# Pairs of 256-column products become single 512-column products

## The chip, the cores and the metric

The kernel runs on one core of a Trainium2 chip. Its time is what the device takes for one launch, in microseconds. Three runs of the kernel before took 2214.0, 2215.96 and 2220.0 us (median 2215.96). One more execution was profiled; all rows below come from it.

## The reference

Two small transformers run one after the other on 256 tokens of width 1024, all in fp32. The first has two layers; each is a gated feed-forward block, a token mixing block and a second feed-forward block:

```
h = h + 0.5*g1*swiglu(modulate(rms_norm(h)), wg, wu, wd)        # d_ff 2816
h = h + g2*token_mixing(modulate(rms_norm(h)), w_in, ...)       # two attentions, a gate, w_o
h = h + 0.5*g3*swiglu(modulate(rms_norm(h)), wg', wu', wd')
```

The second takes this result and a second stream of 256 context tokens. Its layer 0 runs retention and a gated scan on both streams, an output product, and an MLP of width 4096 with squared ReLU, again on both. Its layer 1 is a windowed attention and such an MLP on the first stream alone. The shifts, scales and gates (18 vectors of the first, 16 of the second part) are products of three conditioning vectors with weights of their own.

## The kernel before

**Tiling.** Activations are kept transposed: a list of four tiles, each with two blocks of 128 features (k) by 256 tokens. Every fp32 operand is split into two rounded halves, `h` and `l`, and each product is three products (`mm3`, line 849): hh, hl, lh. A weight tile of 512 KB is loaded into an `f4` slot by SP's queue, rounded by ScalarE (`CAST r<-f`) and subtracted by VectorE (`TENSOR_TENSOR r<-f,r`), so that it occupies two `r4` slots (`wload`, line 825). `wcols` (line 835) loads 256 columns of a weight as two tiles of four k.

**Two kinds of product.** `tr_product` (line 854) holds 128 weight columns still and lets 256 tokens pass: its result is transposed, one 128x512 PSUM bank for 256 weight columns. `nat_product` (line 864) holds 128 tokens still and lets 256 weight columns pass; t numbers the two blocks of 128 tokens. Both have 24 products of 256 columns for one half of a bank (8 k times 3). The down products (`down`, `half`) already pass 512 columns. PSUM has four banks `gu` and four `acc`.

**Stages.** The labels are 0ffn1, 0mix, 0ffn2, 1ffn1, 1mix, 1ffn2 (first part, `feed` and `mixing`), ret (`retention_gla`), out (`half`), jmlp (`joint_mlp`), win (`window`), mlp (`feed`). A stage ends in a tail: for each t the residual, the norm and four transposes, mostly on VectorE. The next stage starts with products by token block, which need only t = 0 while the tail of t = 1 runs: `by_tile` in the feed-forwards (two slices p of 256 columns) and the queries in mixing and win. In ret and jmlp the streams are `"c"` (context) and `"x"`; each passes through every weight tile in its own products.

**Order.** The engines' orders are not the code's. Each call is recorded as an operation with a cost; products into one bank join up to 1400 ns. A planner (`Plan.schedule`, line 255) then lays the operations out over PE, ACT, DVE, POOL and SP with modelled times, takes the earliest-recorded ready one first, and gives each tile one of the slots in `SLOTS`. What is printed by `order` is that fixed sequence. On the chip an engine never leaves its sequence. Background units (`bg`: `ma<-mw`, one 512 KB tile for the conditioning vectors) are spread over the stages.

Because every call goes through line 506, all instructions have that line, and the rows are told apart by tile names: `r` split halves, `f` raw weights, `b` half-width work tiles, `ma`/`mw` conditioning, `resx` the residual.

Of the kernel before, what the change touches and what calls it, by code (L numbers as in the profile page):

```python
# [15 lines left out]
ALU = mybir.AluOpType  # L16
# [13 lines left out]
SLOTS = {"r4": 26, "f4": 7, "mw": 2, "ma": 3, "b2": 17, "p256": 4, "p128": 5, "p16": 12, "pb": 2}  # L30
# [9 lines left out]
VERBOSE = False  # L40

# [394 lines left out]
class _Engine:  # L436
# [3 lines left out]
    def __getattr__(self, what):  # L440
# [3 lines left out]
        def call(*args, **kw):  # L444
# [62 lines left out]

            plan.record(eng, issue, outs, ins, dur, nbytes, table, share)
# [67 lines left out]
def two_blocks_kernel(ctx: ExitStack, tc: tile.TileContext, A: dict, out: bass.AP, dumps=None):  # L576
# [248 lines left out]
    def wload(ap, a, b):  # L825
        l = r4()[:, : a * b].rearrange("p (a b) -> p a b", a=a)
        r = f4()[:, : a * b].rearrange("p (a b) -> p a b", a=a)
        load(r, ap)
# [13 lines left out]

    def ahead(*which):

        for W, c0 in which:
            ws = wcols(W, c0)
            stash[W.tensor.name, W.offset, c0] = ws
# [6 lines left out]
    def tr_product(ps, nT, ws, nk=KT):  # L854

        for b in range(2):
            o = ps[:, b * T : b * T + T]
            c = slice(b * P, b * P + P)
            for k in range(nk):
                wh, wl = ws[k // 4]  # L860
                nh, nl = nT(k)
                mm3(o, wh[:, k % 4, c], wl[:, k % 4, c], nh, nl, k == 0, k == nk - 1)

    def nat_product(o, nT, ws, t):

        tt = slice(t * P, t * P + P)
        for k in range(KT):
            wh, wl = ws[k // 4]
            nh, nl = nT(k)
            mm3(o, nh[:, tt], nl[:, tt], wh[:, k % 4, :], wl[:, k % 4, :], k == 0, k == KT - 1)  # L870
# [12 lines left out]
    def kpairs(tiles):  # L883


        def f(k):
            c = slice((k % 2) * T, (k % 2) * T + T)
            return tiles[k // 2][0][:, c], tiles[k // 2][1][:, c]

        return f  # L890
# [118 lines left out]
    def gated(nT, wg, wu):  # L1009


        def whole(p):
            pg, pu = gu(), gu()
            tr_product(pg, nT, wcols(wg, p * 256))
            tr_product(pu, nT, wcols(wu, p * 256))
            sg, hd = b2(), b2()
            nc.scalar.activation(sg, pg, AF.Silu)
            nc.vector.tensor_mul(hd, sg, pu)
            return kpairs([split(hd, 0.5)])

# [12 lines left out]

        return lambda p: by_tile(p) if p < NAT else whole(p)

    def squared(nT, w1):
        def whole(p):
            ps = gu()
            tr_product(ps, nT, wcols(w1, p * 256))
            hd = b2()  # L1040
            nc.scalar.activation(hd, ps, AF.Relu)
            nc.scalar.activation(hd, hd, AF.Square)
            return kpairs([split(hd)])

        def by_tile(p):
            ws = wcols(w1, p * 256)
            h = pair()
            for t in range(2):
                ps = gu()
                nat_product(ps[:, 0:T], nT, ws, t)  # L1050
                hd = pl([P, T])
                nc.scalar.activation(hd, ps[:, 0:T], AF.Relu)
                nc.scalar.activation(hd, hd, AF.Square)
                put([h], 0, t, transposed(gu(), hd))
            return kpairs([h])

        return lambda p: by_tile(p) if p < 2 else whole(p)
# [144 lines left out]
    def mixing(l, nT, m, rate, before, tail, after=()):  # L1202
# [21 lines left out]
        def dv(c):  # L1224
            ps = gu()
            ws = wcols(W, 1792 + c * 256)
            for t in range(2):
                nat_product(ps[:, t * T : t * T + T], nT, ws, t)
            nc.scalar.copy(vd[:, :, c * 256 : c * 256 + 256], ps.rearrange("p (t c) -> p t c", t=2))
# [222 lines left out]
    def retention_gla(nT, lgam, between):  # L1452
# [6 lines left out]
        def pr_T(c0):  # L1459
            ws = wcols(W, c0)  # L1460
            ps = {}
            for n in both:
                ps[n] = gu()
                tr_product(ps[n], nT[n], ws)
            return ps

        def pr_N(c0):

            v = {n: [b2(), b2()] for n in both}
            for c in range(2):  # L1470
                ws = wcols(W, c0 + c * 256)
                for n in both:
                    ps = gu()
                    for t in range(2):
                        nat_product(ps[:, t * T : t * T + T], nT[n], ws, t)
                    for t in range(2):
                        copy = nc.scalar.copy if t == 0 else nc.vector.tensor_copy
                        copy(v[n][t][:, c * 256 : c * 256 + 256], ps[:, t * T : t * T + T])
            return v

        def silu(c0):

            g = {}
            for b in range(2):
                ps = pr_T(c0 + b * 256)
                for n in both:
                    g[n, b] = b2()
                    nc.scalar.activation(g[n, b], ps[n], AF.Tanh, scale=0.5)
                    nc.vector.scalar_tensor_tensor(g[n, b], g[n, b], 1.0, ps[n], ALU.add, ALU.mult)
# [173 lines left out]
        pq = pr_T(1536)  # L1663
        qb, kb = {}, {}
        for n in both:
            qb[n] = b2()
            nc.scalar.mul(qb[n], pq[n], 0.125)
        pk = pr_T(1792)
        for n in both:
            kb[n] = b2()  # L1670
            nc.scalar.copy(kb[n], pk[n])
# [138 lines left out]
    def joint_mlp(nT, w1, w2, x, gates, before, tail, after, stats):  # L1810

        hid = {}

        def hidden(*ps):
            ws = {p: wcols(w1, p * 256) for p in ps}
            for n in ("c", "x"):
                for p in ps:
                    o = gu()
                    tr_product(o, nT[n], ws[p])
                    hd = b2()  # L1820
                    nc.scalar.activation(hd, o, AF.Relu)
                    nc.scalar.activation(hd, hd, AF.Square)
                    hid[n, p] = split(hd)
# [5 lines left out]
        for r in range(4):  # L1829
            mine = {n: kpairs([hid[n, 4 * r + i] for i in range(4)]) for n in ("c", "x")}  # L1830
# [10 lines left out]
    def window(nT, ctx, consts, before, tail, after):  # L1841
# [9 lines left out]
        def queries(half, t, ws):  # L1851
            pq[half, t] = acc()
            for c in range(2):
                nat_product(pq[half, t][:, c * 256 : c * 256 + 256], nT, ws[c], t)
# [26 lines left out]
        ws = [wcols(W, c * 256) for c in range(2)]  # L1881
# [14 lines left out]
        def more_queries():  # L1896
            ws = [wcols(W, 512 + c * 256) for c in range(2)]
            for t in range(2):
                pq[1, t] = gu()
                for c in range(2):  # L1900
                    nat_product(pq[1, t][:, c * 256 : c * 256 + 256], nT, ws[c], t)
# [122 lines left out]
    for l in range(2):  # L2024
# [9 lines left out]
        feed(gated(kpairs(nT), A["ffn_wg"][l, 0], A["ffn_wu"][l, 0]), A["ffn_wd"][l, 0], 11, RATE if l else FIRST, before, closing(*keys, n2), [(A["w_in"][l], 0), (A["w_in"][l], 256)], lead=0 if l else LEAD)  # L2034
# [4 lines left out]
        mixing(l, kpairs(n2), hold["m"], RATE / 3, lambda: get(*keys), closing(*keys, n3), [(A["ffn_wg"][l, 1], 0), (A["ffn_wu"][l, 1], 0)])  # L2039
# [6 lines left out]
        else:  # L2046
            cT, xT = new_T(), new_T()

            def before():
# [6 lines left out]
                for t in range(2):  # L2056
                    normed(cT, t, xc[t], None, V["Csc1_0"], V["Csh1_0"])
# [8 lines left out]
            def tail(t, accs):  # L2066
# [3 lines left out]
                normed(xT, t, xs[t], r, V["Xsc1_0"], V["Xsh1_0"])  # L2070
# [4 lines left out]
        feed(gated(kpairs(n3), A["ffn_wg"][l, 1], A["ffn_wu"][l, 1]), A["ffn_wd"][l, 1], 11, RATE, before, tail, [(A["ffn_wg"][1, 0], 0), (A["ffn_wu"][1, 0], 0)] if l == 0 else [(A["ev_w_in_2"][0], 0), (A["ev_w_in_2"][0], 256)])  # L2075
# [6 lines left out]
    y = retention_gla({"c": kpairs(cT), "x": kpairs(xT)}, hold["lgam"], lambda: bg(1))  # L2082

    def ln_tail(n, t, st, nxt, G, SH, g, b):
        mean, r = moments(st)
        normed(nxt, t, x[n][t], r, G, SH, mean=mean)
        affine(x[n][t], mean, r, g, b)
# [7 lines left out]
    nxt, maps = {}, {}  # L2095
    for n in both:
# [3 lines left out]
        nxt[n] = new_T()  # L2100
    half(y, A["ev_w_out_2"][0], 0, 1, ALPHA, x, gates, lambda n, t: ln_tail(n, t, stats[n, t], nxt[n], *maps[n], g, b), [(A["mlp_w1_2"][0], 0)], stats)
# [5 lines left out]
    nT = {n: kpairs(nxt[n]) for n in both}  # L2107
# [53 lines left out]
    def tail(t, accs):  # L2161
        st = new_stats()
        residual(xs[t], accs, V["Xg1_1"], t, ALPHA, stats=st)
        ln_tail("x", t, st, last, *lastmap["m"], *lastmap["l"])

    window(kpairs(nx2["x"]), ctx_keys, consts, before, tail, [(A["mlp_w1_2"][1], 0), (A["mlp_w1_2"][1], 256)])
# [59 lines left out]
```

## Time and profile before

| | |
|---|---|
| median of three runs | 2215.96 us (2214.0 to 2220.0) |
| profiled execution | 2215.32 us, span 2213.5 us |
| mean granted TensorE clock | 0.984 |
| TensorE busy | 2109.6 us (95%) |
| VectorE, ScalarE busy | 1594.7 us (72%), 999.8 us (45%) |
| read from HBM | 447.11 MB, 203 GB/s over the span |

Read it from the engine that is nearly always busy: its busy share by stage, then what one of its instructions costs where it never waits (start of one row to the start of the next), then the places where it does wait and for whom.

### The profile page before, as it was taken

Reading aid. Unit: us, or ns where it says so; the run is one execution under the profiler, and the core shown is the slowest. Engines: PE = TensorE matmul, PEld = TensorE weight load, DVE = VectorE, ACT = ScalarE, POOL = GpSimd, SP = SyncE. Lnnn points to the kernel's source line nnn. Section 1 sums busy time; section 2 is a strip of 40 time slices with the busy share of each in tenths; the row PEclk is TensorE's granted clock in tenths of the full one; section 3 lists DMA queues with packets and bytes.
Section 4 is the critical chain, followed back from the end, with each engine's and each line's share of the span. In section 5 each row is a group of like instructions: output and inputs, shape, how many; then the busy total and the mean of one; then the engine's idle time right before and its main releaser. Section 6 shows DMA issues by size and latency. Waiting matters only on the chain. (4 is left out here: it accounts for less than half of the span.)

```text
span 2213.5 us, 37030 instructions
## 1 busy us (share of the span) xinstructions
PE 2109.6 (95%) x14996; PEld 1911.0 (86%) x14996; DVE 1594.7 (72%) x2111; ACT 999.8 (45%) x1525; POOL 53.7 (2%) x51
## 2 busy tenths in 40 slices
PE   7999799999999999999999899979999999989998
PEld 4999798899989998988998798868998898978997
DVE  6777887886687669899789965559653536878545
ACT  3544355454444445565445326423333332365552
POOL 0000100000000000000000010000000000000000
PEclk8999999999999999999999999989999999999999
DMA  9988867698868874776797543244642423244661
GB/s 347 353 265 319 267 203 238 216 303 272 271 224 295 273 240 143 230 246 224 252 315 239 165 144 99 100 137 133 205 150 86 162 86 126 73 139 130 205 215 55
DMA packets 282084, 450.73 MB, mean 204 GB/s; under 512 B 17164, under 2 KB 203692, under 8 KB 281912
## 3 DMA queue, kind: packets, MB, share of 16 engines
q1 hardware_dynamic: 281912, 448.37, 61.4%
q8 instruction: 117, 1.92, 0.4%
q14 instruction: 55, 0.45, 0.1%
HBM read 447.11 MB, written 1.20 MB: 203 GB/s over the span
## 5 line engine op out<-in xcount | busy, mean ns | idle before, releaser
L506 PE MATMUL gu<-r,r 128*128 128x256 f32 (+1 forms) x9776 | 1224.0, 286 | 8.7 <-DVE r L506 5.3
L506 PEld LDWEIGHTS gu<-r,r 128*128 128x128 f32 (+1 forms) x9776 | 1196.6, 193 | 30.9 <-issue 12.0
L506 ACT CAST r<-f 128x1024 fp32r<-128x1024 f32 x545 | 566.5, 1051 | 651.7 <-PE acc L506 133.8
L506 DVE TENSOR_TENSOR r<-f,r 128x1024 fp32r<-128x1024 f32 x545 | 652.4, 1221 | 207.4 <-PE gu L506 80.6
L506 PE MATMUL acc<-r,r 128*128 128x512 f32 (+3 forms) x3408 | 721.8, 375 | 21.7 <-ACT b L506 12.8
L506 PEld LDWEIGHTS acc<-r,r 128*128 128x128 f32 (+1 forms) x3408 | 574.7, 189 | 138.3 <-ACT b L506 14.3
L506 DVE SCALAR_TENSOR_TENSOR ma<-mw,sc_all,ma 128x1024 f32<-128x1024 f32 x252 | 320.3, 1281 | 106.6 <-DMA mw<-in_ada_w 60.7
L506 ACT CAST r<-gu 128x256 fp32r<-128x256 f32 (+2 forms) x130 | 42.9, 387 | 150.7 <-PE gu L506 150.7
L506 DVE TENSOR_TENSOR r<-b,r 128x512 fp32r<-128x512 f32 (+1 forms) x74 | 46.1, 632 | 82.4 <-ACT r L506 82.1
L506 POOL TENSOR_TENSOR p<-p,mhalf 128x1 f32<-128x1 f32 (+2 forms) x42 | 51.0, 1217 | 2154.9 <-DVE p L506 2154.9
L506 ACT ACTIVATE b<-gu 128x512 f32<-128x512 f32 x92 | 54.9, 596 | 103.1 <-PE gu L506 102.9
L506 PE MATMUL gu<-ident,b 128*128 128x128 f32 (+1 forms) x448 | 64.6, 287 | 38.0 <-DVE b L506 35.3
L506 PEld LDWEIGHTS gu<-ident,b 128*128 128x128 f32 (+1 forms) x448 | 46.6, 143 | 53.5 <-DVE b L506 46.9
L506 DVE TENSOR_TENSOR b<-acc,b 128x512 f32<-128x512 f32 (+1 forms) x82 | 54.9, 673 | 22.1 <-PE acc L506 21.0
L506 DVE TENSOR_TENSOR b<-b,b 128x512 f32<-128x512 f32 (+2 forms) x97 | 63.1, 668 | 7.4 <-DMA b<-mod_Csc 2.2
L506 ACT ACTIVATE b<-acc,p 128x256 f32<-128x256 f32 (+1 forms) x96 | 51.6, 548 | 23.0 <-DVE p L506 18.2
L506 ACT ACTIVATE ma<-mw,sc_all 128x1024 f32<-128x1024 f32 x36 | 41.5, 1152 | 40.2 <-DMA mw<-in_ada_w 21.5
L506 DVE SCALAR_TENSOR_TENSOR r<-b,r 128x512 fp32r<-128x512 f32 x44 | 30.3, 689 | 38.0 <-ACT r L506 38.0
L506 DVE TENSOR_TENSOR r<-gu,r 128x256 fp32r<-128x256 f32 (+2 forms) x130 | 49.6, 430 | 5.5 <-ACT r L506 5.2
L506 ACT CAST r<-b 128x512 fp32r<-128x512 f32 (+1 forms) x74 | 41.6, 573 | 13.4 <-DVE b L506 11.9
L506 ACT COPY b<-gu 128x512 f32<-128x512 f32 (+1 forms) x42 | 20.9, 507 | 56.7 <-PE gu L506 37.1
L506 DVE TENSOR_REDUCE p<-acc 128x2 f32<-128x512 f32 (+1 forms) x64 | 42.7, 684 | 2.6 <-PE acc L506 2.4
(122 smaller groups left out, 929.3 us busy)
## 6 DMA issues: line engine op xcount, KB each, us to landing
mw<-in_ada_w SPq DMA_DIRECT2D x128, 512.0 KB
f<-in_mlp_w SPq DMA_DIRECT2D x128, 512.0 KB
mw<-in_w_mod SPq DMA_DIRECT2D x96, 512.0 KB
f<-in_ffn_wg SPq DMA_DIRECT2D x88, 512.0 KB
f<-in_ffn_wu SPq DMA_DIRECT2D x88, 512.0 KB
f<-in_ffn_wd SPq DMA_DIRECT2D x88, 512.0 KB
f<-in_w_in SPq DMA_DIRECT2D x36, 512.0 KB
f<-in_w_gate SPq DMA_DIRECT2D x32, 512.0 KB
```

The lines of the kernel that those rows point to most:

```text
L506: f(*[put(a) for a in args], **{k: put(a) for k, a in kw.items()})
```

## The change

Where two 256-column products have the same stationary operand, one 512-column product takes their place.

1. By token block: `wide` loads 512 weight columns as four tiles of two k by 512 (or 256 columns of `wg` beside 256 of `wu`, with two DMAs of 256 KB a tile), and `nat_product` fills a bank in 24 products of 512 columns in place of 48 of 256: `by_tile` of four `gated` feed-forwards and of mlp, queries and `vd` in mixing, `pr_N` in ret, queries in win.
2. By stream: `new_J` keeps both streams side by side (an `r4` tile for `h`, one for `l`, per two k), and `tr_block` passes all 512 tokens over 128 held weight columns: `pr_T` in ret, and in jmlp every hidden slice but the first two. The first q and k products of ret and the first two slices of jmlp stay one per stream. A bank then holds one block of 128 weight columns for both streams, so `pr_T` hands out 256-column pieces of it.
3. mlp's first two slices are made together; the copies of `vd` and of `pr_N` are 512 wide per token block.
4. `r4` gets 30 slots for 26, `b2` 16 for 17; a scratch region for DMA is cut to 1024 bytes.

Core of the diff:

```diff
-SLOTS = {"r4": 26, "f4": 7, ..., "b2": 17, ...}
+SLOTS = {"r4": 30, "f4": 7, ..., "b2": 16, ...}
+BACC = {"dynamic_dma_scratch_size": 1024}
...
+    def wide(W, c0, W2=None):
...
+        for k0 in range(0, KT, 2):
+            k = slice(k0 * P, (k0 + 2) * P)
+            if W2 is None:
+                ws.append(wload(W[k, c0 : c0 + 512].rearrange("(k p) c -> p k c", p=P), 2, 512))
+            else:
+                ws.append(wload([w[k, c0 : c0 + 256].rearrange("(k p) c -> p k c", p=P) for w in (W, W2)], 2, 512))
...
+    def tr_block(o, nT, ws, c, nk=KT):
+        for k in range(nk):
             wh, wl = ws[k // 4]
             nh, nl = nT(k)
+            mm3(o, wh[:, k % 4, c], wl[:, k % 4, c], nh, nl, k == 0, k == nk - 1)
...
+    def new_J():
+        return [(r4(), r4()) for _ in range(4)]
+    def kstream(tiles, n):
+        def f(k):
+            c = (k % 2) * 2 * T
+            c = slice(c, c + 2 * T) if n is None else slice(c + n * T, c + n * T + T)
             return tiles[k // 2][0][:, c], tiles[k // 2][1][:, c]
...
         def by_tile(p):                                  # gated
-            ws, us = wcols(wg, p * 256), wcols(wu, p * 256)
+            ws = wide(wg, p * 256, wu)
...
-                nat_product(ps[:, 0:T], nT, ws, t)
-                nat_product(ps[:, T : 2 * T], nT, us, t)
+                nat_product(ps, nT, ws, t)
...
-        ws = [wcols(W, c * 256) for c in range(2)]       # mixing; win alike
+        ws = wide(W, 0)
         for t in range(2):
-            for c in range(2):
-                nat_product(pq[t][:, c * 256 : c * 256 + 256], nT, ws[c], t)
+            nat_product(pq[t], nT, ws, t)
...
-        def pr_T(c0):                                    # ret
+        def pr_T(c0, take):
             ws = wcols(W, c0)
-            ps = {}
+            for b in range(2):
+                ps = gu()
+                tr_block(ps, nT["both"], ws, slice(b * P, b * P + P))
+                for i, n in enumerate(both):
+                    take(n, slice(b * T, b * T + T), ps[:, i * T : i * T + T])
...
+            ws = wide(W, c0)                             # pr_N
             for n in both:
-                ps[n] = gu()
-                tr_product(ps[n], nT[n], ws)
...
+                for t in range(2):
                     ps = gu()
+                    nat_product(ps, nT[n], ws, t)
...
+            else:                                        # joint_mlp, hidden(p)
                 for p in ps:
+                    for b in range(2):
+                        o = gu()
+                        tr_block(o, nT["both"], ws[p], slice(b * P, b * P + P))
+                        h, l = squares(o)
+                        for i, n in enumerate(("c", "x")):
+                            hid[n, 2 * p + b] = h[:, i * T : i * T + T], l[:, i * T : i * T + T]
```

**TensorE in jmlp.** The first fence is the kernel before, at the end of one bank (`gu_118`) and the start of the next; `r_94` and `r_86` are weight tiles (both halves of a pair share a name, and `x2` is hh and hl).

```order
L506 MATMUL gu_118<-r_78,r_94 128x256 x2
L506 MATMUL gu_118<-r_78,r_79 128x256
L506 MATMUL gu_118<-r_78,r_94 128x256 x2
L506 MATMUL gu_118<-r_78,r_79 128x256
L506 MATMUL gu_115<-r_83,r_86 128x256 x2
L506 MATMUL gu_115<-r_83,r_93 128x256
L506 MATMUL gu_115<-r_92,r_86 128x256 x2
```

The second is the changed kernel at such a place; `r_97` and `r_77` hold the h and the l of both streams.

```order
L507 MATMUL gu_120<-r_97,r_74 128x512
L507 MATMUL gu_120<-r_77,r_74 128x512
L507 MATMUL gu_120<-r_97,r_98 128x512
L507 MATMUL gu_119<-r_72,r_89 128x512
L507 MATMUL gu_119<-r_76,r_89 128x512
L507 MATMUL gu_119<-r_72,r_69 128x512
```

A bank takes 24 rows of one 512-column product where it took 48 products of 256 columns.

**TensorE in the tail of 1ffn2.** Before: the last products of the context stream's q and k for ret (`gu_118`), and the two transposes of t = 1 (`ident`, from the work tiles `b`).

```order
L506 MATMUL gu_118<-r_78,r_83 128x256
L506 MATMUL gu_118<-r_74,r_82 128x256 x2
L506 MATMUL gu_118<-r_74,r_83 128x256
L506 MATMUL gu_115<-ident_67,b_101 128x128 x4
L506 MATMUL gu_117<-ident_67,b_112 128x128 x4
L506 MATMUL gu_115<-r_94,r_69 128x256 x2
```

After: the same two transposes, behind products of `pr_N` on the context stream (`gu_121`).

```order
L507 MATMUL gu_118<-ident_67,b_115 128x128 x4
L507 MATMUL gu_121<-r_77,r_91 128x512
L507 MATMUL gu_121<-r_87,r_91 128x512
L507 MATMUL gu_121<-r_77,r_70 128x512
L507 MATMUL gu_119<-ident_67,b_109 128x128 x4
L507 MATMUL gu_118<-ident_67,b_116 128x128 x4
L507 MATMUL gu_121<-r_86,r_94 128x256
```

What fills the tail differs: between the last down product of t = 0 and the first transposes of t = 1 stand 18 down products and 96 of 256 columns before, 12 down products, 26 of 256 and 24 of 512 columns after. The other 70 products of q and k now stand ahead of the last down products.

## Rows read from the trace of the kernel before

**Rows 1.** Page, part 1: busy time, share of the span, instructions.

```profile
PE 2109.6 (95%) x14996; PEld 1911.0 (86%) x14996; DVE 1594.7 (72%) x2111; ACT 999.8 (45%) x1525; POOL 53.7 (2%) x51
```

**Rows 2.** Windows: span, busy by engine (instructions), granted clock, DMA share, GB/s.

```profile
39.00:246.00 207.00, 194.71 (x1347) 180.30 (x1347) 157.64 (x174) 97.49 (x112) 1.52 (x1) 0.97 0.91 313
...
831.00:1022.00 191.00, 180.90 (x1446) 164.30 (x1443) 175.00 (x244) 105.31 (x199) 10.63 (x6) 1.00 0.66 213
...
1246.00:1468.00 222.00, 203.15 (x1673) 188.11 (x1673) 136.67 (x206) 95.13 (x166) 7.55 (x6) 0.95 0.39 125
...
1526.00:1892.00 366.00, 365.61 (x2341) 332.20 (x2341) 204.93 (x256) 132.50 (x178) 3.95 (x4) 1.00 0.41 133
1892.00:1982.00 90.00, 83.64 (x756) 72.51 (x756) 74.91 (x149) 45.88 (x104) 0.00 (x0) 1.00 0.38 127
```

**Rows 3.** Timeline of PE in jmlp: start, duration, instructions.

```profile
1567.72 21.95 PE L506 MATMUL acc<-r,r 128*128 128x512 f32 x96
1589.50 5.91 PE L506 MATMUL gu<-r,r 128*128 128x256 f32 x48
1595.35 1.06 PE L506 MATMUL gu<-ma,ones 128*32 128x512 f32 x8
1596.34 17.54 PE L506 MATMUL gu<-r,r 128*128 128x256 f32 x144
1613.72 0.63 PE L506 MATMUL acc<-r,r 128*128 128x512 f32 x2
```

**Rows 4.** Timeline of PE in mlp.

```profile
2098.84 5.92 PE L506 MATMUL gu<-r,r 128*128 128x256 f32 x48
2104.60 5.63 PE L506 MATMUL acc<-r,r 128*128 128x512 f32 x24
2110.06 5.92 PE L506 MATMUL gu<-r,r 128*128 128x256 f32 x48
```

**Rows 5.** Timeline of PE at the end of 0ffn1.

```profile
222.53 4.27 PE L506 MATMUL acc<-r,r 128*128 128x512 f32 x18
233.77 2.58 PE L506 MATMUL acc<-r,r 128*128 128x512 f32 x5 [6.97 <-ACT r L506]
```

**Rows 6.** Timeline of ACT at that place.

```profile
226.63 1.04 ACT L506 CAST r<-f 128x1024 fp32r<-128x1024 f32 x1 [4.08 <-DMA f<-in_w_in]
```

**Rows 7.** Timelines of PE in the tail of 1ffn2.

```profile
1216.02 7.39 PE L506 MATMUL acc<-r,r 128*128 128x512 f32 x30 [0.95 <-ACT r L506]
...
1236.25 1.00 PE L506 MATMUL gu<-r,r 128*128 128x256 f32 x7
1244.41 1.11 PE L506 MATMUL gu<-ident,b 128*128 128x128 f32 x4 [7.16 <-DVE b L506]
```

**Rows 8.** Timeline of PE in the tail of out.

```profile
1520.72 3.36 PE L506 MATMUL gu<-r,r 128*128 128x256 f32 x26
1525.98 1.40 PE L506 MATMUL gu<-ident,b 128*128 128x128 f32 x8 [1.91 <-DVE b L506]
```

**Rows 9.** Timeline of PE at the end of ret.

```profile
1459.60 2.93 PE L506 MATMUL acc<-r,r 128*128 128x512 f32 x6 [9.86 <-ACT b L506]
```

**Rows 10.** Lines by form: busy, mean ns of one, idle before and its releasers.

```profile
L506 ACT CAST r<-f 128x1024 fp32r<-128x1024 f32 x545 | 566.5, 1051 | 651.7 <-PE acc L506 133.8 <-PE gu L506 126.7 <-DMA f<-in_ffn_wd 90.1
L506 ACT ACTIVATE b<-gu 128x512 f32<-128x512 f32 x92 | 54.9, 596 | 103.1 <-PE gu L506 102.9
L506 ACT COPY b<-gu 128x256 f32<-128x256 f32 x16 | 6.0, 374 | 32.9 <-DVE b L506 15.0 <-PE gu L506 13.7 <-PE acc L506 4.2
L506 DVE TENSOR_TENSOR r<-f,r 128x1024 fp32r<-128x1024 f32 x545 | 652.4, 1221 | 207.4 <-PE gu L506 80.6 <-PE acc L506 63.3 <-issue 29.6
```

**Rows 11.** Waits of PE: total us, times, longest us.

```profile
PE gu L506 <- DVE b L506: 40.0, 31, 7.2
PE acc L506 <- ACT b L506: 13.8, 4, 9.9
PE acc L506 <- ACT r L506: 8.1, 3, 7.0
...
PE gu L506 <- DVE r L506: 5.3, 5, 2.9
```

**Rows 12.** Timeline of SP: one DMA issue.

```profile
1449.41 0.38 SPq L506 DMA_DIRECT2D f<-in_ev_w_out  x1
```

More of the change, by code (lines that the diff above doesn't have):

```diff
@@ L827, in wload @@
         r = f4()[:, : a * b].rearrange("p (a b) -> p a b", a=a)
-        load(r, ap)
+        if isinstance(ap, list):
+            n = b // len(ap)
+            for i, part in enumerate(ap):
+                load(r[:, :, i * n : i * n + n], part)
+        else:
+            load(r, ap)
         h = r4()[:, : a * b].rearrange("p (a b) -> p a b", a=a)
@@ L841, in wcols @@
         return [wload(W[k0 * P : (k0 + 4) * P, c0 : c0 + n].rearrange("(k p) c -> p k c", p=P), 4, n) for k0 in range(0, nk, 4)]
-    def ahead(*which):
-        for W, c0 in which:
-            ws = wcols(W, c0)
-            stash[W.tensor.name, W.offset, c0] = ws
+    def wide(W, c0, W2=None):
+        key = (W.tensor.name, W.offset, c0, "wide")
+        if key in stash:
+            return stash.pop(key)
+        ws = []
+        for k0 in range(0, KT, 2):
[4 more added lines that the diff above has]
+                ws.append(wload([w[k, c0 : c0 + 256].rearrange("(k p) c -> p k c", p=P) for w in (W, W2)], 2, 512))
+        return ws
+    def ahead(*which):
+        for W, c0, *other in which:
+            key = (W.tensor.name, W.offset, c0)
+            if other:
+                stash[(*key, "wide")] = wide(W, c0, *other)
+            else:
+                stash[key] = wcols(W, c0)
     def mm3(o, lh, ll, rh, rl, first, last):
@@ L1043, in whole, with by_tile, hidden @@
             return kpairs([split(hd)])
-        def by_tile(p):
-            ws = wcols(w1, p * 256)
-            h = pair()
+        first = []
+        def by_tile():
+            ws = wide(w1, 0)
+            hs = [pair(), pair()]
             for t in range(2):
                 ps = gu()
-                nat_product(ps[:, 0:T], nT, ws, t)
-                hd = pl([P, T])
-                nc.scalar.activation(hd, ps[:, 0:T], AF.Relu)
+                nat_product(ps, nT, ws, t)
+                hd = b2()
+                nc.scalar.activation(hd, ps, AF.Relu)
                 nc.scalar.activation(hd, hd, AF.Square)
-                put([h], 0, t, transposed(gu(), hd))
-            return kpairs([h])
-        return lambda p: by_tile(p) if p < 2 else whole(p)
+                put(hs, 0, t, transposed(gu(), hd))
+            first.extend(kpairs([h]) for h in hs)
+        def hidden(p):
+            if p == 0:
+                by_tile()
+            return first[p] if p < 2 else whole(p)
+        return hidden
     def feed(hidden, wd, n, rate, before, tail, after=(), lead=0, hold=HOLD):
@@ L1222, in dqk, with dv @@
             dT.append(split(ps, sc))
-        def dv(c):
+        wv = []
+        def dv(t):
+            if t == 0:
+                wv.append(wide(W, 1792))
             ps = gu()
[L1226 to L1229, printed above, removed]
+            nat_product(ps, nT, wv[0], t)
+            nc.scalar.copy(vd[:, t, :], ps)
         def gate(br, fp):
@@ L1662, in retention_gla @@
                 las[n, t] = split(z)
[L1663 to L1671, printed above, removed]
+        qb, kb = [{n: b2() for n in both} for _ in range(2)]
+        pr_T(1536, lambda n, c, ps: nc.scalar.mul(qb[n][:, c], ps, 0.125))
+        pr_T(1792, lambda n, c, ps: nc.scalar.copy(kb[n][:, c], ps))
         between()
@@ L1829, in joint_mlp @@
         for r in range(4):
-            mine = {n: kpairs([hid[n, 4 * r + i] for i in range(4)]) for n in ("c", "x")}
+            mine = {n: lambda k, n=n: hid[n, 8 * r + k] for n in ("c", "x")}
             last = {"stats": stats} if r == 3 else {}
@@ L1852, in queries @@
             pq[half, t] = acc()
-            for c in range(2):
-                nat_product(pq[half, t][:, c * 256 : c * 256 + 256], nT, ws[c], t)
+            nat_product(pq[half, t], nT, ws, t)
         wv = wcols(W, 1280)
@@ L1879, in put_queries @@
                 nc.vector.tensor_sub(ql, pv, qh)
-        ws = [wcols(W, c * 256) for c in range(2)]
+        ws = wide(W, 0)
         for t in range(2):
@@ L1896, in more_queries @@
         def more_queries():
-            ws = [wcols(W, 512 + c * 256) for c in range(2)]
+            ws = wide(W, 512)
             for t in range(2):
                 pq[1, t] = gu()
-                for c in range(2):
-                    nat_product(pq[1, t][:, c * 256 : c * 256 + 256], nT, ws[c], t)
+                nat_product(pq[1, t], nT, ws, t)
                 put_queries(1, t)
@@ L2073, in tail @@
                     nc.vector.scalar_tensor_tensor(xs[t][:, c], xs[t][:, c], r, V["fg"][:, c], ALU.mult, ALU.mult)
[L2075 removed]
+        feed(gated(kpairs(n3), A["ffn_wg"][l, 1], A["ffn_wu"][l, 1]), A["ffn_wd"][l, 1], 11, RATE, before, tail, [(A["ffn_wg"][1, 0], 0, A["ffn_wu"][1, 0])] if l == 0 else [(A["ev_w_in_2"][0], 0), (A["ev_w_in_2"][0], 256)])
     dump("xb1", xs)
@@ L2106, in two_blocks_kernel @@
     gates2 = {n: V[n.upper() + "g2_0"] for n in both}
-    nT = {n: kpairs(nxt[n]) for n in both}
+    nT = {"c": kstream(nxt, 0), "x": kstream(nxt, 1), "both": kstream(nxt, None)}
     nx2, maps2, lnp = {}, {}, []
@@ L2163, in tail @@
         residual(xs[t], accs, V["Xg1_1"], t, ALPHA, stats=st)
-        ln_tail("x", t, st, last, *lastmap["m"], *lastmap["l"])
-    window(kpairs(nx2["x"]), ctx_keys, consts, before, tail, [(A["mlp_w1_2"][1], 0), (A["mlp_w1_2"][1], 256)])
+        ln_tail(None, t, st, last, *lastmap["m"], *lastmap["l"])
+    window(kpairs(nx2["x"]), ctx_keys, consts, before, tail, [(A["mlp_w1_2"][1], 0, None)])
     dump("sx1", xs)
```

81 lines of the change are left out of this document (42 added, 39 removed).

## The prediction

> **What bounds the kernel now.** I began with the busy shares: TensorE works 2109.6 of 2213.5 us, VectorE 72%, ScalarE 45% [rows 1]. So the end of the program moves with TensorE's own work, unless TensorE waits for something that the change doesn't shorten. The stretches tell where that is so [rows 2]: jmlp (1526 to 1892 us) has TensorE busy 365.61 of 366 us, at a granted clock of 1.00 (the 2.4 GHz level), with VectorE at 205 us and DMA at 0.41: nothing but TensorE bounds it. 0ffn1 (39 to 246) has DMA at 0.91, and ret (1246 to 1468) has 19 us in which TensorE stands still. 1mix (831 to 1022) has VectorE at 175 of 191 us.
>
> Next the price of one product, from starts in the timeline where nothing waits. In jmlp 96 products of 512 columns fill 1567.72 to 1589.50, 226.9 ns each; 144 of 256 columns fill 1596.34 to 1613.72, 120.7 ns each [rows 3]. In mlp, where the two kinds take turns, 48 of 256 fill 5.76 us (120.0 ns) and 24 of 512 fill 5.46 us (227.5 ns) [rows 4]. Twice 256 columns thus cost 240.0 to 241.4 ns, once 512 columns 226.9 to 227.5 ns. A part that doesn't grow with the columns is paid once for a product, and a pair that becomes one saves 12.5 to 14.5 ns. I take 13.5.
>
> Last the places where TensorE waits, since work saved ahead of a wait may be handed back there: the longest are 6.97 us at the end of 0ffn1 for a rounding on ScalarE [rows 5], itself behind a weight that came 4.08 us late [rows 6]; 7.16 us in the tail of 1ffn2 for VectorE's norm [rows 7]; 9.86 us at the end of ret [rows 9]. In total TensorE waits 40.0 us for `b` tiles of VectorE, mostly tails [rows 11].
>
> **The change part by part.**
>
> *Products removed.* Pairs, counted from the loops, 24 to a bank:
> - four gated feed-forwards, two slices, two token blocks: 4 x 2 x 2 x 24 = 384;
> - two mixings, queries and vd: 2 x 4 x 24 = 192;
> - ret, six `pr_T` of two banks and two `pr_N` of four: 288 + 192 = 480;
> - jmlp, 14 slices of two banks: 672;
> - win, four query banks: 96; mlp, two banks: 48.
>
> That is 1872 pairs, so 1872 products and as many weight loads go. 1872 x 13.5 ns = 25.3 us (23.4 to 27.1 by the two ends). jmlp's share is 672 x 13.5 = 9.1 us, and it is kept whole: no wait follows there for 366 us.
>
> No clean run of 512-column products in a `gu` bank stands in the trace; the rows for 512 columns are of the down products into `acc`. I price the new ones alike, since the columns, the rows held and the types are the same. If they cost twice 256 columns, the gain is nothing.
>
> *What is handed back.*
> - 0ffn1: 96 pairs, 1.3 us. DMA is 0.91 busy, and its end is a wait behind a late weight [rows 2, 5, 6]. The same bytes come, so I take all of it as lost.
> - Tail of 1ffn2. Between the last down product of t = 0, from which VectorE's chain runs, and the transposes of t = 1, TensorE had 18 x 0.227 + 96 x 0.120 = 15.6 us of work, then waited 7.16 us [rows 7]. Now it has 12 x 0.227 + 26 x 0.120 + 24 x 0.227 = 11.3 us. VectorE's chain there has the same adds, norms and about as many background units and weight subtractions among them, so the wait grows by 4.3 us. The 70 products that moved ahead cover the 0.95 us wait of the last down products for their weights [rows 7]. Net 3.3 us lost.
> - Tail of out. Between the two last pairs of transposes stood 26 products and a wait of 1.91 us [rows 8]; now there are 48, 22 x 0.120 = 2.6 us more, so I take this wait as gone: 1.9 us won.
> - Other tails: 59 products of 256 columns (7.1 us) stood ahead of the first transposes of t = 1, now 36 of 512 (8.2 us) or 24 of 512 and 22 of 256 (8.1 us). There is still more to do for t = 0, so the saving is kept. Within a us either way, taken as 0.
> - ret: 6.5 us, of which I take a quarter (1.6) as lost, since its last part is a chain over ScalarE, VectorE and late weights. The wait of 9.86 us [rows 9] has five roundings of late weights queued ahead of the copy that frees the bank on ScalarE, and the new sequence has them there too: unchanged.
> - win and mlp: 1.3 and 0.65 us, a third to a half of it inside tails: 0.7 lost.
>
> *Weights.* Bytes and 512 KB tiles are the same, so rounding (1051 ns) and subtraction (1221 ns) are too [rows 10]. But `pr_N` used two tiles for 11.5 us and then the next two; now the first bank goes through four tiles in 24 x 0.227 = 5.4 us, and VectorE needs 4 x 1.22 = 4.9 us for them: no cover left if they were not split beforehand. Eight `r4` slots are then held through all banks. Against this stand four more `r4` slots. Bounds: 0, and 2.9 us for each wide group, the longest wait of a `gu` product for a subtraction [rows 11]; I take 0, as such waits come to 5.3 us in all now. Below nothing: more slots can take these and the waits of `acc` for ScalarE's roundings (8.1 us) away, 13.4 us.
>
> *Small work.* Six `pr_T` have four pieces of 256 columns in place of two of 512: on ScalarE 4 x 374 - 2 x 596 = 304 ns each [rows 10], about 2 us in ret, where it works 95 of 222 us; VectorE likewise. 32 DMAs more at 0.38 us of SP's time [rows 12] are 12 us over 2200. Hidden behind TensorE, 0; uncovered they would cost 2 us. One `b2` slot less: 0 to a few us, taken as 0.
>
> *Sum.* -25.3 + 1.3 + 3.3 - 1.9 + 1.6 + 0.7 = -20.3 us against the profiled execution's 2215.3: 2195. That execution lies 0.6 us under the median, which I neglect.
>
> **The rivals.**
>
> *Only the bound stage gains.* Everything outside jmlp is filler between chains and is handed back: 2215.3 - 9.1 = 2206. For it: 1mix's VectorE and 0ffn1's DMA are nearly full, and every stage begins with such products inside a tail [rows 2, 11]. Against: the fillers don't run out in most tails.
>
> *More slots help as well.* Half of the 13.4 us of waits for splits [rows 11] go: 2188. Against: the longest of these is DMA's lateness [rows 6], which slots alone don't mend.
>
> *Wide groups stall (slower).* Each of the 17 groups (8 in the feed-forwards, 4 in mixing, 2 in ret, 2 in win, 1 in mlp) waits at its second tile for VectorE's subtraction: 17 x 2.9 = 49 us at the worst, 2215.3 - 20.3 + 49 = 2244. It decides from 9 groups on, where it has eaten 25 us. For it: VectorE at 0.92 in 1mix and its fixed sequence. Against: the groups at a stage's start are loaded ahead, and the sums of such waits are small now.
>
> *No saving in a pair.* The new products take as long as two: 2215. Against it are the rows of both kinds, side by side in two stages [rows 3, 4]. The Trainium skill (TensorE: Matmul & The Clock Gate, section Back-to-back issue gap) has a rule on this side: a product alone takes its columns at the array's clock and about 2.5 ns more. By that the change would save 1872 x 2.5 ns = 4.7 us, an estimate from that page, and end at 2211. The trace doesn't agree: 120.0 ns for 256 columns is 13.3 ns above the 106.7 that 2.4 GHz gives [rows 4], and 226.9 is 13.6 above 213.3 [rows 3].
>
> **How the numbers follow.** The forecast, 2195 with its own range 2187 to 2204 (the ends of the saving and 6 us for waits that the new order makes or removes), has 0.62. Only jmlp gains: 0.15. Slots help: 0.13. Wide groups stall: 0.05. No saving: 0.05. The range for 8 in 10 reaches from 2183, a little under the third case, to 2209, above the second. Less than 0.3% (6.6 us) can't be told from no change, so faster means below 2209.3: all of the forecast and of the third case and two thirds of the second, some 0.85; same gets the rest of that and the fifth, 0.10; slower 0.05.
>
> **What would show it.** 512-column products into `gu` at 226 to 228 ns between starts in jmlp, and jmlp some 9 us shorter, show the price; other spacing shows it wrong. TensorE's busy time should fall by about 25 us to 2085 and its instructions by 1872. A wait of about 11 us in the tail of 1ffn2, and none in that of out, show the two tails; waits of `gu` products for VectorE's `r` tiles at the start of wide groups, summing to more than 15 us, would show the slower rival. If TensorE's busy time falls by 25 us and the span by less than 12, the saving was handed back to chains that I took as covered.

## The result: 2179.59 us, ratio 0.983

| | before | after |
|---|---|---|
| median (range) | 2215.32 us (2214.0 to 2220.0) | 2179.59 us (2175.03 to 2182.66) |
| ratio, 95% interval | | 0.9833 (0.981 to 0.9857) |
| profiled execution, span | 2215.32, 2213.5 us | 2175.03, 2173.3 us |
| TensorE busy | 2109.6 us | 2082.8 us |
| span less TensorE busy | 103.9 us | 90.5 us |

The gain is 35.7 us; 20.3 were forecast, and the time lies 3 us below the range. The direction was right. TensorE's busy time fell by 26.8 us, as forecast. (The profiled execution after is the shortest of its four, 4.6 us under their median, so a few us of what its rows show are its own.) The other part is idle time of TensorE, 13.4 us less in these two executions, where the forecast had put some 5 us more.

Part 1 of the page after, against [rows 1]:

```profile
PE 2082.8 (96%) x13124; PEld 1804.9 (83%) x13124; DVE 1592.1 (73%) x2115; ACT 994.3 (46%) x1527; POOL 52.4 (2%) x51
```

1872 products fewer, as counted. VectorE and ScalarE do what they did before, to within 6 us.

TensorE's timeline in jmlp after, where the new products stand beside the old down products (start, duration):

```profile
1605.27 21.92 PE L507 MATMUL gu<-r,r 128*128 128x512 f32 x96
...
1629.75 19.20 PE L507 MATMUL acc<-r,r 128*128 128x512 f32 x84
1648.79 21.92 PE L507 MATMUL gu<-r,r 128*128 128x512 f32 x96
1670.55 21.92 PE L507 MATMUL acc<-r,r 128*128 128x512 f32 x96
1692.31 21.92 PE L507 MATMUL gu<-r,r 128*128 128x512 f32 x96
```

From 1648.79 to 1670.55 are 96 new products, 226.7 ns each, exactly what the down products beside them take and what [rows 3] gave. The price was read off the right row.

The stretches after, each from the last transposes of one tail to those of the next (span, busy by engine, granted clock, DMA share, GB/s), in the order 0ffn1, 1ffn2, ret, jmlp; the same stretches of the kernel before stand below them:

```profile
36.60:254.60 218.00, 206.74 (x1311) 184.82 (x1312) 171.91 (x193) 106.26 (x129) 2.98 (x2) 0.96 0.92 312
1021.90:1240.30 218.40, 206.60 (x1378) 186.67 (x1376) 186.51 (x222) 100.65 (x135) 2.98 (x2) 0.98 0.74 242
1240.30:1451.60 211.30, 194.97 (x1201) 160.71 (x1202) 134.62 (x214) 94.31 (x176) 9.61 (x8) 0.97 0.40 129
1502.50:1860.50 358.00, 357.04 (x1685) 297.36 (x1686) 206.18 (x260) 129.19 (x178) 3.95 (x4) 1.00 0.42 136
```

```profile
37.10:257.60 220.50, 206.91 (x1435) 192.09 (x1436) 170.34 (x192) 105.22 (x129) 2.98 (x2) 0.96 0.89 304
1032.60:1245.80 213.20, 201.95 (x1422) 185.22 (x1422) 182.93 (x221) 104.05 (x138) 2.98 (x2) 0.99 0.78 253
1245.80:1474.40 228.60, 209.75 (x1705) 193.64 (x1705) 140.47 (x213) 96.42 (x169) 9.53 (x8) 0.95 0.39 125
1526.00:1894.70 368.70, 367.72 (x2357) 334.11 (x2358) 207.63 (x260) 135.00 (x183) 3.95 (x4) 1.00 0.40 132
```

jmlp is 10.7 us shorter. 1ffn2 and ret have to be read together, since 24 of ret's products (5.4 us) now stand in the tail of 1ffn2: 441.8 became 429.7 us. Idle time is the span less the first busy figure: 18.9 us in ret before, 16.3 after.

TensorE's waits after (total us, times, longest), against [rows 11]:

```profile
PE gu L507 <- DVE b L507: 34.8, 26, 6.4
PE acc L507 <- ACT b L507: 11.6, 2, 8.8
PE acc L507 <- ACT r L507: 6.6, 3, 4.7
...
PE gu L507 <- DVE r L507: 3.8, 5, 1.2
```

All four classes shrank, none by more than 5.2 us. Single waits of 0.8 us and more were 36 in the timeline before and are 27 after. No one wait explains the surplus.

### The profile page after: what moved, and what is told of

It reads as the page before. It is cut to its first block, busy times and chain, and to the rows that moved or that the text cites. A ratio compares the mean times of both kernels' runs of the same rounds, so it can differ in the third digit from the quotient of the medians.

```text
span 2173.3 us, 33312 instructions
## 1 busy us (share of the span) xinstructions
PE 2082.8 (96%) x13124; PEld 1804.9 (83%) x13124; DVE 1592.1 (73%) x2115; ACT 994.3 (46%) x1527; POOL 52.4 (2%) x51
## 2 busy tenths in 40 slices
DMA packets 273367, 450.51 MB, mean 207 GB/s; under 512 B 17677, under 2 KB 185773, under 8 KB 273209
## 4 chain that ended last, share of the span: by engine, by line
PE 66%; DVE 15%; DMA 11%; issue 3%; ACT 3%; POOL 0%; SPq 0%; DVEq 0%; ACTq 0%; POOLq 0%
PE gu L507 42%; PE acc L507 24%; DVE b L507 5%; DVE r L507 4%; DMA mw<-in_ada_w 3%; DVE ma L507 2%; DMA f<-in_ffn_wu 2%; DVE p L507 2%; ACT r L507 2%; DMA f<-in_ffn_wd 1%; DMA mw<-in_w_mod 1%; DVE resx L507 1%; DMA f<-in_w_in 1%; DMA f<-in_ev_w_out 1%; ACT b L507 1%
## 5 line engine op out<-in xcount | busy, mean ns | idle before, releaser
L507 PE MATMUL gu<-r,r 128*128 128x256 f32 (+2 forms) x8048 | 1197.8, 309 | 6.9 <-DVE r L507 3.8
L507 PEld LDWEIGHTS gu<-r,r 128*128 128x128 f32 (+1 forms) x8048 | 1093.3, 192 | 95.8 <-issue 12.0
L507 PEld LDWEIGHTS acc<-r,r 128*128 128x128 f32 (+1 forms) x3264 | 568.2, 189 | 142.8 <-ACT b L507 12.3
L507 ACT ACTIVATE b<-gu 128x512 f32<-128x512 f32 (+1 forms) x104 | 56.5, 554 | 143.6 <-PE gu L507 126.0
L507 ACT CAST r<-b 128x512 fp32r<-128x512 f32 (+1 forms) x74 | 41.6, 573 | 11.8 <-DVE b L507 10.1
```

The source lines that it names most:

```text
L507: f(*[put(a) for a in args], **{k: put(a) for k, a in kw.items()})
```

## The experiments

**The price alone.** The same sequence on every engine, but each new product is handed to TensorE as two halves.

```diff
             def issue():
...
+                if halve:
+                    for c in (slice(0, 256), slice(256, 512)):
+                        g = {"start": q["start"] and c.start == 0, "stop": q["stop"] and c.start > 0}
+                        f(o[0][:, c], **{**q, **g, "rhs": q["rhs"][:, c]})
+                    return
...
```

`halve` is set for the new 512-column products alone; `o` and `q` hold what the product is called with.

> The changed kernel, with the same sequence on every engine, but each of its 1872 new 512-column products is given to TensorE as two of 256 columns. Theory A (a pair saves 13.5 ns, and the rest of the gain comes from slots and the new sequence): about 1872 x 13.5 = 25 us over the changed kernel's 2179.6, so 2204 (2200 to 2208); some 11 us of the gain stay. Theory B (all of the gain is the products' price, with the clock's level as part of it): back to 2213 to 2217. Rival C (the price is handed back to chains and the gain is sequence alone): under 2190.

2204.14 us (2202.59 to 2206.78; the kernel before, measured beside it, 2214.7): 24.55 us slower than the changed kernel, 13.1 ns for each of the 1872 pairs. Theory A holds, B and C fall. jmlp is 366.9 us here and 358.0 in the changed kernel: 8.9 us for 672 pairs, 13.2 ns each. The other 10.6 us of the gain stay without the price. Its page, part 1:

```profile
PE 2108.7 (96%) x14996; PEld 1911.4 (87%) x14996; DVE 1593.5 (72%) x2115; ACT 993.0 (45%) x1527; POOL 52.4 (2%) x51
```

The busy time is that of before again, to within a microsecond, but the span is 2202.8: TensorE stands still for 94.1 us in place of 103.9. These 9.8 us are the surplus.

**Slots alone,** with the smaller scratch region, in the kernel before.

```diff
-SLOTS = {"r4": 26, ..., "b2": 17, ...}
+SLOTS = {"r4": 30, ..., "b2": 16, ...}
...
-    nc = bacc.Bacc("TRN2", target_bir_lowering=False, num_devices=1)
+    nc = bacc.Bacc("TRN2", target_bir_lowering=False, num_devices=1, dynamic_dma_scratch_size=1024)
```

> The kernel before with 30 r4 slots and 16 b2 slots, and the smaller scratch region, all else as it was. Theory A1 (of the 11 us beyond the price, the four slots bring most): 2202 to 2208. Rival A2 (they come from the sequence and from joined work, the slots are only there so that the wide groups fit): 2213 to 2217.

2214.53 us (2210.79 to 2221.45), ratio 1.0002 (0.9991 to 1.0014), idle 107.8 us. A1 falls. The other way round, the changed kernel with 28 slots:

> The changed kernel with 28 r4 slots in place of 30 (28 is the least with which its wide groups fit), another sequence for it. If the ten us of waits that went beyond the price hang on spare slots: 2184 to 2190. If not: 2175 to 2184, as with any other sequence of this kernel.

2182.9 us (2181.49 to 2186.09), idle 93.7: inside the lower bracket, though 3 us slower. Spare slots aren't what brings the 10 us.

**Is it the luck of a sequence?** The planner turns any small change of its costs into another order on all engines. Two more sequences of the kernel before, one of the changed kernel:

```diff
-    WRITE = {"PE": 158.0, ...}         # redraw 1
+    WRITE = {"PE": 170.0, ...}
-                dur = 69.0 + ...       # redraw 2, VectorE
+                dur = 72.0 + ...
```

> The kernel before, computing the same with the same products, slots and bytes; only the planner's figure for the delay after a product is 170 ns in place of 158, so that it lays out another sequence. Theory S (the 10 us beyond the price belong to the change): within 4 us of the kernel before, 2211 to 2219. Theory L (they are the luck of one sequence among many): 5 us or more away on either side.

> The kernel before again, with the planner's fixed cost of a VectorE instruction at 72 ns in place of 69: a second other sequence of the same work. Theory S: 2211 to 2219. Theory L: 5 us or more from 2214.7, on either side.

> The changed kernel with the same other figure (72 ns for 69), another sequence of the changed kernel's work. Theory S: 2176 to 2184. Theory L: 5 us or more from 2179.6, most likely slower, up to 2190, which is what price alone gives.

2208.7 us (ratio 0.9967, 0.9953 to 0.9981), 2220.93 (1.0025, 1.0012 to 1.0039) and 2177.01 (0.9829, 0.9812 to 0.9847); the kernel before, measured beside them, 2215.94. By the letter of the expectations the first two speak for theory L: 7.2 us under it and 5.0 over it. So one sequence of this kernel says little about a few microseconds. But four sequences of the old work (with that of the slots) have a mean of 2214.9 us and 103.8 us of idle time, and five of the changed one (itself, its redraw, that with 28 slots, and the two at the end of this section) lie between 2177.0 and 2182.9, mean 2179.9, idle 92.5; the last three have edits of their own, and the first two alone have a mean of 2178.3. Price alone would give 2190.4. None of the nine lies between 2183 and 2208. The surplus belongs to the change, and luck makes it uncertain by some 3 us.

**Which half?** The change with one of its halves undone, each in three sequences (two with the redraws' figures).

```diff
-            ws = wide(wg, p * 256, wu)          # stream alone: by_tile, queries,
+            ws, us = wcols(wg, p * 256), wcols(wu, p * 256)   # vd, pr_N, win, mlp
...
-                tr_block(ps, nT["both"], ws, slice(b * P, b * P + P))   # block alone:
+                tr_product(ps, nT[n], ws)                             # pr_T, jmlp
```

> The changed kernel without its part by token block (weights in tiles of four k by 256 everywhere): only the part by stream stays, 288 pairs in ret and 672 in jmlp. Price alone: 960 x 13.5 = 13 us. With the slots' theory A1 another 8 to 10: 2191 to 2195. By A2, and if the surplus of ret (17.3 us where 6.5 were priced) sits in its products by stream: 2192 to 2196 with ret's end early and the stages before it unchanged; if it sits in the wide products: 2201 to 2204.

> The part by stream alone, in another sequence (the planner's delay after a product at 170 ns for 158). Price alone, from 2214.8 as the mean of four sequences of the old work: 960 x 13.1 = 12.6 us, 2202. If the 10 us of waits belong to this half: 2192 (its first sequence was 2196.2); if to the other half: 2202; a half of them: 2197. Each 5 us either way for the sequence.

> The part by stream alone, in a third sequence (the fixed cost of a VectorE instruction at 72 ns for 69, with which the kernel before was 5 us slower and the changed kernel 2.6 us faster). 2192, 2197 or 2202 as with the one before.

> The changed kernel without its part by stream (each stream passes in products of its own in ret and jmlp): only the part by token block stays, 912 pairs. Price alone 12.3 us, less about 3 us handed back in 0ffn1 and in the tail of 1ffn2. By A1 (slots bring 8 to 10): 2195 to 2199. By A2 without slots' share: 2204 to 2207.

> The part by token block alone, in another sequence (170 ns for 158). Price alone: 912 x 13.1 = 11.9 us, 2203. If the 10 us of waits belong to this half: 2193; if to the other: 2203 (its first sequence was 2205.7); a half of them: 2198. Each 5 us either way.

> The part by token block alone, in a third sequence (72 ns for 69): 2193, 2198 or 2203 as with the one before.

| | times, us | mean | price alone | beyond it | idle, mean |
|---|---|---|---|---|---|
| old work, 4 sequences | 2215.3, 2214.5, 2208.7, 2220.9 | 2214.9 | | | 103.8 |
| stream alone | 2196.2, 2204.1, 2192.5 | 2197.6 | 2202.3 | -4.7 | 99.1 |
| token block alone | 2205.7, 2200.8, 2195.7 | 2200.7 | 2202.9 | -2.2 | 99.6 |
| both, 5 sequences | 2179.6, 2177.0, 2182.9, 2181.4, 2178.4 | 2179.9 | 2190.4 | -10.5 | 92.5 |

Price alone is 2214.9 less 13.1 ns for 960, 912 and 1872 pairs. Neither half has the 10 us to itself: the idle time falls by 4.7 and 4.2 us with one half, by 11.3 with both. The kernel before took 2218.1 us when measured beside the four redraws of the halves, and 2214.7 to 2215.9 us beside all others. Taken as gains over the kernel before beside each, the means are 19.4 us for stream alone, 16.2 for token block alone and 35.3 for both (0.6 for the four of the old work), which is 6.2, 3.6 and 10.1 us beyond price: so read, the halves add up to the whole. Three sequences give a mean only to about 3 us, so the split between the halves stays open. The first sequence of each, taken alone, would have misled: 2196.2 against 2205.7, where the means are 3 us apart.

**ret's share.**

```diff
-                tr_block(ps, nT["both"], ws, slice(b * P, b * P + P))   # pr_T
+                tr_product(ps, nT[n], ws)
...
-            ws = wide(W, c0)                                            # pr_N
+                ws = wcols(W, c0 + c * 256)
```

> The changed kernel with the old products in ret alone (each stream by itself in all pr_T, weights of pr_N in tiles of four k by 256): 480 pairs come back. At the price that the halved kernel gave, 24.55 / 1872 = 13.1 ns a pair, that is 6.3 us: 2186 (2184 to 2188). If the sequence of ret and of the tail before it, 12 us shorter together where 6.3 are price, hangs on these products: 2190 to 2194. If it comes from the sequence planned for the wide groups elsewhere: under 2184.

2188.0 us (2186.35 to 2190.18): 8.4 us slower than the changed kernel, 6.3 by price. It ends at the upper edge of the first bracket, and the 2 us over lie inside the sequences' spread. Price alone would give 2196.7 us for the 1392 pairs that this kernel keeps, so 8.7 us of surplus stay without ret's products: ret doesn't hold most of it.

**How far the price goes down.** Quarters in place of halves.

```diff
-                    for c in (slice(0, 256), slice(256, 512)):
+                    for c in [slice(i, i + 128) for i in range(0, 512, 128)]:
```

> The changed kernel with each of the 1872 new products given as four of 128 columns, same sequence. If the price is a fixed part of every product, some 13.1 ns beside 0.4167 ns a column, each wide product takes 4 x 66.5 = 266 ns for 227: 1872 x 39 ns = 73 us, 2250 to 2256. Rival: a short product can't start before the held block of the next is loaded, so that it has a floor: well above, with 80 ns a product 1872 x 93 = 174 us, 2354.

The two executions took 2643.2 and 2795.0 us, at mean granted clocks of 0.959 and 0.905. Both expectations were too low. The second was profiled; TensorE's timeline in its jmlp, and that stretch as a window:

```profile
2214.66 4.92 PE L514 MATMUL acc<-r,r 128*128 128x512 f32 x21
2219.42 42.77 PE L512 MATMUL gu<-r,r 128*128 128x128 f32 x382
```

```profile
2219.42:2260.00 40.58, 40.58 (x365) 40.58 (x364) 8.08 (x10) 9.16 (x13) 0.00 (x0) 1.00 0.14 39
```

At a granted clock of 1.00 a product of 128 columns takes 40.58 / 365 = 111 ns, hardly less than one of 256 (120.0). In this window the engine's weight loads (second figure) are busy all the time. The fixed part of 13 ns holds between 256 and 512 columns; it would make 66 ns a product at 128 columns, where 111 were measured. 4 x 111 - 227 = 217 ns for 1872 products would be 406 us of the 464 that the shorter execution took more than the changed kernel. What the other 58 are stays open: there is no trace of that execution, and its mean granted clock was lower too (0.959, in the changed kernel 0.984 to 0.986).

**The longest wait that is left.** TensorE waits 8.81 us at ret's end, behind roundings of late weights on ScalarE (9.86 us before [rows 9]). The row, and the 2.7 us behind the wait as a window:

```profile
1437.73 2.93 PE L507 MATMUL acc<-r,r 128*128 128x512 f32 x6 [8.81 <-ACT b L507]
```

```profile
1437.73:1440.46 2.73, 2.73 (x6) 2.16 (x7) 2.73 (x4) 1.94 (x2) 0.00 (x0) 0.50 0.06 21
```

This wait costs more than its length: when TensorE goes on, the granted clock is 0.50 (the 1.2 GHz level), and the six products take 455 ns each, twice the 226.7 of jmlp. The edit puts those roundings behind the copies that free the banks.

```diff
+                    nc.gate = nc.ops[-1].idx     # the last copy of a bank in ret
...
-            return wload(...)
+            w = wload(...)                       # a chunk of out's weights
+            if nc.label == "out":
+                nc.ops[-2].deps.add(nc.gate)     # its rounding, for the planner
+            return w
```

> The changed kernel with one edge more for the planner: the roundings of out's weights come behind the last copies of ret's PSUM banks on ScalarE, so that the wait of 8.81 us at ret's end has no rounding of a late weight queued ahead of the copy it waits for. If that queue is the cause: 5 to 7 us, 2173 to 2175, with ret's end that much earlier (other stages as the new sequence has it, 3 us either way). Rival: the weights land late in any case and out's products wait for them in its place: 2177 to 2182.

2181.35 us (2179.98 to 2185.01): nothing won. The end of ret and the tail of out in this kernel:

```profile
1432.95 0.46 PE L507 MATMUL gu<-b,p 64*64 64x64 f32 x16
1434.40 0.71 PE L507 MATMUL acc<-b,b 128*128 128x128 f32 x4 [0.99 <-DVE b L507]
```

```profile
1481.59 1.11 PE L507 MATMUL gu<-ident,b 128*128 128x128 f32 x4 [4.52 <-DVE b L507]
...
1493.00 1.32 PE L507 MATMUL gu<-ident,b 128*128 128x128 f32 x8 [1.29 <-DVE b L507]
```

The wait of 8.81 became 0.99, so its cause was read rightly. But 4.52 us came up in the tail of out for VectorE's norm (0.63 in the changed kernel): from the end of 1ffn2 to the end of out it is 264.6 us here and 262.2 there. VectorE shows why, in this kernel and then in the changed one, just ahead of that norm:

```profile
1469.14 7.79 DVE L507 TENSOR_TENSOR b<-b,b 128x512 f32<-128x512 f32 x12
```

```profile
1470.38 4.06 DVE L507 TENSOR_TENSOR b<-b,b 128x512 f32<-128x512 f32 x6
```

The planner put twelve operations there where six stood, 3.7 us more. And from 1481.59 to 1495.45 the granted clock is 0.83, where it is 1.00 in the changed kernel (1479.09 to 1491.00). The time fits the rival, but the rival named the weights; it was VectorE. The second edit:

```diff
+                nc.late = AFFINE     # in the tail of 1ffn2
                 for j in range(2):
...
                     nc.vector.scalar_tensor_tensor(xs[t][:, c], xs[t][:, c], r, V["fg"][:, c], ...)
+                nc.late = 0
```

> As the one before, and in the tail of 1ffn2 the four scalings of the residual (0.75 us each on VectorE) come behind the norm of t = 1, so that the chain of VectorE that ends in the wait of 6.45 us is 1.5 us shorter: a wait of about 5 us there, 1 to 2 us less than the one before. Rival: nothing, since VectorE is filled with other background work instead.

2178.41 us (2173.49 to 2180.22); the wait there is 6.17 us for 6.45.

```profile
1241.59 1.12 PE L507 MATMUL gu<-ident,b 128*128 128x128 f32 x4 [6.17 <-DVE b L507]
```

VectorE does two of the scalings where it did a background unit before, in its own wait for the norm's root. The rival holds: the time is 2.9 us under that of the first edit, which 0.28 us of wait don't explain and the spread of sequences does, and neither edit beats the changed kernel beyond the spread of sequences.

## Why the prediction was wrong

**Products removed, -25.3.** Right: 24.55 by the halved kernel, 13.1 ns a pair for 13.5. The rival of no saving falls. So do the 4.7 us by the rule of the Trainium skill (TensorE: Matmul & The Clock Gate, section Back-to-back issue gap): the measurement decides.

**What is handed back, +5.0. This is the step that failed**, with the terms set to 0 beside it: together they should have been some -10, and the sign was wrong. The forecast asked of each wait what the lost cover would add to it, and kept everything else in its place, but for 6 us either way that its range had for waits that the new order makes or removes. In the new sequence everything else moved too, and the runs lie some 15 us from its +5.0.

- *0ffn1, +1.3.* The wait behind the late weight didn't grow; it shrank from 6.97 [rows 5]:

```profile
222.62 4.27 PE L507 MATMUL acc<-r,r 128*128 128x512 f32 x18
231.63 2.79 PE L507 MATMUL acc<-r,r 128*128 128x512 f32 x5 [4.74 <-ACT r L507]
```

 The stage's idle time is 10.7 to 15.0 us in four kernels with the change (itself, halved, its redraw, without ret's part) and 13.1 to 15.6 in the four sequences of the old work. A stage with DMA at 0.92 varies more than the term was worth; a loss of 1.3 isn't shown.

- *Tail of 1ffn2, +3.3.* The products ahead and behind stand as counted, and the wait was to be about 11 us. Against [rows 7], TensorE after, and then the start and the end of VectorE's part:

```profile
1214.81 4.71 PE L507 MATMUL acc<-r,r 128*128 128x512 f32 x20
1219.35 3.27 PE L507 MATMUL gu<-r,r 128*128 128x256 f32 x26
1224.75 0.66 PE L507 MATMUL gu<-ident,b 128*128 128x128 f32 x4 [2.13 <-DVE b L507]
...
1231.00 1.43 PE L507 MATMUL gu<-r,r 128*128 128x512 f32 x5 [0.81 <-DVE r L507]
1238.87 1.11 PE L507 MATMUL gu<-ident,b 128*128 128x128 f32 x4 [6.45 <-DVE b L507]
```

```profile
1217.34 0.68 DVE L507 TENSOR_TENSOR b<-acc,b 128x512 f32<-128x512 f32 x1
...
1238.12 0.69 DVE L507 TENSOR_TENSOR b<-b,b 128x512 f32<-128x512 f32 x1
```

 The kernel before: what TensorE did behind the rows shown ahead, and the same part of VectorE with what stood in front of it:

```profile
1223.25 5.43 PE L506 MATMUL gu<-r,r 128*128 128x256 f32 x44
1229.70 0.66 PE L506 MATMUL gu<-ident,b 128*128 128x128 f32 x4 [1.01 <-DVE b L506]
```

```profile
1217.81 1.22 DVE L506 TENSOR_TENSOR r<-f,r 128x1024 fp32r<-128x1024 f32 x1
1218.94 1.28 DVE L506 SCALAR_TENSOR_TENSOR ma<-mw,sc_all,ma 128x1024 f32<-128x1024 f32 x1
1221.07 1.28 DVE L506 SCALAR_TENSOR_TENSOR ma<-mw,sc_all,ma 128x1024 f32<-128x1024 f32 x1 [0.85 <-DMA mw<-in_w_mod]
1222.28 0.68 DVE L506 TENSOR_TENSOR b<-acc,b 128x512 f32<-128x512 f32 x1
...
1243.66 0.69 DVE L506 TENSOR_TENSOR b<-b,b 128x512 f32<-128x512 f32 x1
```

 The last down product of t = 0 ended 18 x 0.227 = 4.1 us ahead of 1223.25 before, at 1219.2, and 12 x 0.227 = 2.7 us ahead of 1219.35 after, at 1216.6. VectorE began its part 3.1 us later before (a subtraction and two background units were in front, one of them late by 0.85 us) and 0.7 us later after; the part itself takes 22.1 and 21.5 us. So VectorE is through 25.2 us after that product before and 22.2 after, 3.0 us sooner than "about as many background units and weight subtractions among them" assumed. The three waits sum to 9.4 us, where 0.95, 1.01 and 7.16 stood before: 0.3 us more, not 3.3.

- *Tail of out, -1.9.* Right: the wait of 1.91 us [rows 8] is 0.40 now, and out's idle time is 1.1 us in the changed kernel, halved or not, for 2.1 to 4.1 in four sequences of the old work.

```profile
1496.12 5.99 PE L507 MATMUL gu<-r,r 128*128 128x256 f32 x48
1502.51 1.32 PE L507 MATMUL gu<-ident,b 128*128 128x128 f32 x8 [0.40 <-DVE b L507]
```

- *ret, +1.6.* The wait at its end stayed, as forecast (8.81 for 9.86). A loss isn't shown: without its products the kernel is 8.4 us slower, for 6.3 by price.

- *win and mlp, +0.7.* Not shown. In the means of the same two groups of four, idle time is 5.5 us for 5.1 in win and 8.8 for 9.6 in mlp.

- *Terms at 0 (other tails, weights, small work).* Idle time of 0mix is 6.4 to 9.5 us in four kernels with the change and 10.0 to 11.7 in four sequences of the old work, with no forecast for it at all. The waits of products for subtractions [rows 11] fell from 5.3 to 3.8 us; the wide groups don't stall.

**The rivals.** Only jmlp gains (2206) falls: 15.7 of the 24.55 us of price come from other stages. Wide groups stall falls by the row above. More slots help as well (2188) was nearest in size, but its cause isn't there: slots alone are 0, and of the 13.4 us of waits of which it had half gone, 3.0 are. The range ended at 2183, a little under that case: 6 us for the new order were too few around a sum that had the other sign.

What stays open is what in the change brings the fewer waits: fewer, longer products in the planner's list, or what came with them. The joined copies, mlp's first two slices made together, and the wide tiles, which are read in fewer packets (273367 DMA packets for 282084), were tried by no run alone. The packets are hardly all of it, as stream alone has the old ones (282076) and lies 4.7 to 6.2 us beyond price. The effect is spread: in the means of four kernels with the change and of four sequences of the old work, idle time falls by 3.3 us in 0mix, 1.9 in 1ffn2, 1.8 in out, 1.3 in 0ffn1 and 0.8 in mlp. Which half brings which of these the runs don't tell.

## What to carry to other kernels

Price a removed instruction where its engine never waits, and test it with the sequence held fixed: issuing the new work in the old pieces separates the price from everything that a new order brings. Where a planner lays out the order, one sequence is a draw: here a neutral figure moved the time 7 us down or 5 us up, so effects of that size need several sequences of each side, and a forecast needs that spread in its range, and beside it what a change of the work itself may do to all waits. A wait that is taken out is a gain only if nothing comes up in its place: here 8.81 us at the end of ret became 0.99, and 4.52 came in the next tail, where the planner had put more work in front of the norm. Look for the second in line before calling it a gain.

## What the runs showed of the hardware

A product of 128 columns with fp32r operands takes 111 ns at a granted clock of 1.00 (the quartered kernel), one of 256 columns 120.0 [rows 4] and one of 512 columns 226.7 (jmlp after): from 256 columns to 128 hardly anything is saved. That the load of the held block sets the 111 ns is the likely reading (weight loads were busy throughout), not one that was tested by itself. After 8.81 us in which TensorE stood still, the granted clock was 0.50 and a product of 512 columns took 455 ns (the changed kernel, 1437.73 to 1440.46).
